# A SwiGLU layer in three token groups: sums of weight blocks and normed activations kept in device memory for later groups

## The chip, the cores and the metric

The kernel runs on one core of a Trainium2 chip. The metric is the time of the whole program on the device in microseconds (us); lower is better. Five engines work side by side and wait for each other through semaphores: TensorE (PE in the profile, with its weight loads as PEld), VectorE (DVE), ScalarE (ACT), GpSimd (POOL) and SyncE (SP), which here issues every DMA.

## The reference, cut to what matters

One layer over 2048 + 64 tokens with a width of 1024. The first part (a combined input projection, three mixers, an output projection) is the same in both kernels. The change lies in the second part, a SwiGLU feed-forward block over the result `x`:

```python
h2 = rms_norm(x, lw["ffn_norm"])                         # per token, gain per channel
ff = jax.nn.silu(h2 @ lw["w_gate"]) * (h2 @ lw["w_up"])  # 1024 -> 2816, twice
x = x + ff @ lw["w_down"]                                # 2816 -> 1024
```

Everything is fp32, and the outputs must be fp32-accurate.

## The kernel before, in words

**Arithmetic.** Each fp32 operand is split into a high part (a cast to the fp32r type, on ACT) and a low part, the difference (`rest` on POOL at L86 for weights, L1067 on DVE or POOL for activations). A product is three matmuls, high x high, high x low and low x high (`mm3`). The gate and up projections also use the Strassen-Winograd scheme: an output block pair of 2x2 blocks is made from 7 products instead of 8 (`seven`), each of a weight block or a sum of weight blocks (a11, s2, a12, s1, s3, s4, a22) with a block or a sum of blocks of the normed activations (b11, t2, b21, t1, t3, b22, t4). A product is 4 k steps of 3 matmuls of 128x352, so 84 matmuls make a projection for one pair.

**Loops.** The feed-forward block walks three token groups (`gi`, 704 tokens each) and, in each, 11 pairs of 128-wide blocks of the hidden width (`p`). For a pair the code writes `gate(p)` (84 matmuls), `DN(p-1)`, the down projection of the pair before (96), and `up(p)` (84); `DN(10)` comes last in its group. That is 264 matmuls for a pair and 2904 for a group.

**Weights.** `wsum(p, j)` (L1106 to L1131) is called for every gate (j = 0) and every up (j = 1) in every group. It loads two tiles of 512 KB from `w_gu` (L1109, tile `x2`, 3 buffers, shared with the down weights), forms s1, s3, s2 and s4 on DVE (L1121, L1122, L1123, L1128, in this order), and makes 7 pairs of a cast (L1114) and a rest (L86) into tiles `w` (8 buffers). The sum at L1128 overwrites a12, so it has to wait for the rest of a12 on POOL. `DN` loads 512 KB of down weights per half (L1207), casts it (L1209) and takes its rest (L86, 128x1024).

**Activations.** `HB` holds the seven activation blocks of one group as high and low parts, each 128 x 4 x 352, written in place for the next group. `H2(gi, k, ...)` fills the k-th quarter of all seven: two loads of 352 KB from `x1all` into the one buffer `xh` (L1058), two scalings on DVE (L1059), four sums on DVE (L1072 to L1078), seven casts on ACT (L1065) and seven lows on POOL and DVE (L1067). For groups 1 and 2 the four calls of H2 are written inside `DN(10)` of the group before, one ahead of each of its first four output blocks. Since a quarter goes into all seven blocks, a product of full depth needs all four calls.

**Evictions.** Sums of products leave PSUM on DVE (L1146, L1173, L1188), the up side is multiplied in at L1189 and split into `ah` and `al` (L1191 on ACT, L1192 on DVE), and each piece of the down projection is added into `acc` on DVE (L1221). PSUM gives `gu` 5 buffers and `dn` 3.

**Order.** A scheduler in the framework fixes the order of instructions on each engine when the program is built. Each engine then runs its own list in order, and SP issues the DMAs in order.

Of the kernel before, what the change touches and what calls it, by code (L numbers as in the profile page):

```python
# [3 lines left out]
def prm(n,d):  # L4
    return type(d)(PRM.get(n,d))
# [7 lines left out]
F32 = mybir.dt.float32  # L13
# [8 lines left out]
P = 128  # L22
# [27 lines left out]
def hybrid_layer(ctx: ExitStack, tc: tile.TileContext, x_all, x_t, w_in, w_out, w_gu, w_dn, par, gates, poolw,  # L50
# [56 lines left out]
    x1row = dram.tile([1, T], F32, name="x1row")  # L107

# [663 lines left out]
    ORD0 = "P0 A0 v0 P1 p0 S G0 m0 L0 p1 R0 L1 m1 l0 B0 n0 l1 A1 n1 b0 G1 A2 R1 B1 G2 A3 R2 b1 G3 X Q0 R3 Q1 q0 K0 u0 q1 K1 u1 k0 V w0 k1 w1 v"  # L772
    ORD1 = "A0 S G0 A1 R0 G1 A2 R1 B0 G2 A3 R2 B1 G3 X Q0 b0 R3 Q1 q0 b1 K0 u0 q1 K1 u1 k0 V w0 k1 w1 v"
    ORD3 = "A0 G0 A1 R0 G1 A2 R1 B0 G2 A3 R2 b0 B1 G3 b1 R3"
# [3 lines left out]
    def IN(g):  # L778
# [9 lines left out]
        o = PRM[o].replace("_", " ") if o in PRM else {"o0": ORD0, "o1": ORD1, "o3": ORD3}[o]  # L788
# [195 lines left out]
    def OUT(ci, last=None):  # L984
# [36 lines left out]
        def stat(ps=None, po=po):  # L1021
# [25 lines left out]
          for k in ("b11", "b21", "b22", "t1", "t2", "t3", "t4")}  # L1047
# [54 lines left out]
    def raw():  # L1102
        return pf.tile([P, 1024], F32, name="x2", bufs=3)

    def wsum(p, j):

        r = [raw(), raw()]
        for e in range(2):
            sp.dma_start(r[e], w_gu[2 * p + e, :, j, :])  # L1109
        a11, a12, a21, a22 = r[0][:, :512], r[0][:, 512:], r[1][:, :512], r[1][:, 512:]  # L1110

        def parts(src):
            w = pf.tile([P, 2, 512], F32R, name="w", bufs=prm("b_wg", 8))
            act.copy(w[:, 0, :], src)  # L1114
            rest(w[:, 1, :], w[:, 0, :], src)
            return w

        W = {}
        W["a11"] = parts(a11)
        s1 = pf.tile([P, 512], F32, name="s1", bufs=1)  # L1120
# [9 lines left out]
        W["a22"] = parts(a22)  # L1130
        return W  # L1131

# [35 lines left out]
    def gate(p):  # L1168
# [7 lines left out]
        seven(wsum(p, 0), use)  # L1176
        return s

    def up(p, s):
# [14 lines left out]
        seven(wsum(p, 1), use)  # L1194
        acts[p] = res

    for gi in range(3):
# [4 lines left out]
        def DN(p, extra=()):  # L1202
            extra = list(extra)
            for half in range(2):
                r = raw()
                src = w_dn[2 * p * P:(2 * p + 2) * P, half * 512:half * 512 + 512].rearrange("(q p) e -> p q e", p=P)
                sp.dma_start(r.rearrange("p (q e) -> p q e", q=2), src)  # L1207
                w = pf.tile([P, 2, 1024], F32R, name="wd", bufs=2)
                act.copy(w[:, 0, :], r)  # L1209
                rest(w[:, 1, :], w[:, 0, :], r)  # L1210
# [16 lines left out]
        for p in range(NF // 2):  # L1227
            s = gate(p)
# [4 lines left out]
            up(p, s)  # L1233
            if p == 0:
                sp.dma_start(acc, x1all[:, :, c0:c0 + GT].rearrange("k p t -> p k t"))
# [103 lines left out]
```

## Time and profile before

| | |
|---|---|
| time, median of 3 runs | 2549.59 us (2541.57 to 2551.30) |
| the profiled execution's own time | 2549.71 us |
| its span | 2547.9 us |
| mean granted TensorE clock | 0.954 of full speed |
| feed-forward block on PE | from 1042.5 us to the end |

The time of an execution is its span and 1.8 us around it. The profile has one line for a group of instructions on one engine at one source line, with the busy time, the mean duration of one, and the idle time of the engine just before them with what ended it. A wait is named "engine line <- releaser": the engine stood still at an instruction of this line until the releaser was done.

### The profile page before, as it was taken

The numbers are of one execution on the slowest core, as the hardware profiler recorded it, in microseconds if no ns is written. First come the engines' busy times: TensorE is split into PE (matmuls) and PEld (weight loads), VectorE is DVE, ScalarE is ACT, GpSimd is POOL, SyncE is SP. The second block draws the span as 40 slices with busy tenths as digits, with TensorE's granted clock in tenths as the row PEclk, the third lists the DMA queues.
The fourth block names the chain that finished last, engine by engine and source line by source line (L and its number), as shares of the span: only waits on it lengthen the run. The fifth ranks groups of instructions, "written<-read, shape, count | busy, mean of one in ns | idle before, by whom it ended". The sixth has DMA issues, their size and how long they took to land. (4 is left out here: it accounts for less than half of the span.)

```text
span 2547.9 us, 37616 instructions
## 1 busy us (share of the span) xinstructions
PE 2337.3 (92%) x14158; PEld 2212.8 (87%) x14158; DVE 1690.7 (66%) x2711; ACT 962.6 (38%) x1780; POOL 1097.4 (43%) x788
## 2 busy tenths in 40 slices
PE   5877898989989999899999997999999979999999
PEld 5875767778768999799999996999999979999999
DVE  4457377497789744476666687666676777666665
ACT  3435254355565422333333233323232333333331
POOL 3433013131121133565555555555565555555552
PEclk8888899999999999899999998999999989999999
DMA  7796575765746354422212124212222242222212
GB/s 265 204 256 214 164 241 182 223 197 181 227 129 183 110 152 126 143 92 67 83 63 83 63 90 158 85 60 83 66 75 75 81 153 82 75 75 67 83 60 78
DMA packets 169553, 324.38 MB, mean 127 GB/s; under 512 B 30444, under 2 KB 87643, under 8 KB 161435
## 3 DMA queue, kind: packets, MB, share of 16 engines
q1 hardware_dynamic: 169370, 321.98, 40.1%
q8 instruction: 112, 1.84, 0.3%
q14 instruction: 71, 0.57, 0.1%
HBM read 256.38 MB, written 63.37 MB: 125 GB/s over the span
## 5 line engine op out<-in xcount | busy, mean ns | idle before, releaser
L86 POOL TENSOR_TENSOR w<-x,w 128x512 fp32r<-128x512 f32 x396 | 545.1, 1396 | 533.0 <-ACT w L1114 520.7
L78 PE MATMUL dn<-ah,wd 128*128 128x352 f32 x2112 | 563.8, 326 | 38.2 <-DVE acc L1221 24.6
L78 PE MATMUL gu<-ht,w 128*128 128x352 f32 x2112 | 549.8, 325 | 0.0
L78 PE MATMUL mm<-hTh,w 128*128 128x512 f32 (+3 forms) x1632 | 444.6, 350 | 32.9 <-DVE raw L304 17.5
L78 PE MATMUL gu<-hb,w 128*128 128x352 f32 x1584 | 421.9, 327 | 35.5 <-ACT hb L1065 21.5
L1114 ACT CAST w<-x 128x512 fp32r<-128x512 f32 x396 | 238.2, 616 | 563.5 <-PE gu L78 308.8
L78 PEld LDWEIGHTS dn<-ah,wd 128*128 128x128 f32 x2112 | 378.6, 189 | 49.1 <-DVE acc L1221 33.6
L78 PEld LDWEIGHTS gu<-ht,w 128*128 128x128 f32 x2112 | 378.9, 190 | 0.9 <-ACT w L1114 0.8
L78 PEld LDWEIGHTS mm<-hTh,w 128*128 128x128 f32 x1632 | 297.9, 199 | 66.3 <-DVE raw L304 18.2
L78 PE MATMUL gu<-lt,w 128*128 128x352 f32 x1056 | 343.2, 326 | 0.1
L78 PE MATMUL dn<-al,wd 128*128 128x352 f32 x1056 | 342.5, 324 | 0.0
L1221 DVE TENSOR_TENSOR acc<-dn,acc 128x352 f32<-128x352 f32 x528 | 266.6, 520 | 104.7 <-PE dn L78 104.5
L78 PEld LDWEIGHTS gu<-hb,w 128*128 128x128 f32 x1584 | 287.0, 191 | 38.7 <-ACT hb L1065 23.0
L78 PE MATMUL mm<-hTl,w 128*128 128x512 f32 (+3 forms) x816 | 282.6, 347 | 0.0
L78 PE MATMUL gu<-lb,w 128*128 128x352 f32 x792 | 260.6, 329 | 4.3 <-POOL lb L1067 2.5
L78 PEld LDWEIGHTS gu<-lt,w 128*128 128x128 f32 x1056 | 200.2, 190 | 1.1 <-DVE lt L1067 0.6
L78 PEld LDWEIGHTS dn<-al,wd 128*128 128x128 f32 x1056 | 200.0, 189 | 1.0 <-DVE al L1192 1.0
L86 POOL TENSOR_TENSOR wd<-x,wd 128x1024 fp32r<-128x1024 f32 x66 | 164.5, 2493 | 69.6 <-ACT wd L1209 63.6
L78 PEld LDWEIGHTS mm<-hTl,w 128*128 128x128 f32 x816 | 162.4, 199 | 15.0 <-issue 2.2
L1189 DVE TENSOR_TENSOR s<-s,v 128x352 f32<-128x352 f32 x132 | 169.5, 1284 | 1.4
L657 DVE TENSOR_TENSOR_SCAN C<-z,C,zero 128x512 f32<-128x512 f32 (+4 forms) x148 | 160.2, 1087 | 10.6 <-ACT z L649 9.3
L78 PEld LDWEIGHTS gu<-lb,w 128*128 128x128 f32 x792 | 151.4, 191 | 8.2 <-POOL lb L1067 4.6
(243 smaller groups left out, 3709.6 us busy)
## 6 DMA issues: line engine op xcount, KB each, us to landing
x<-in_w_gu SPq DMA_DIRECT2D x132, 512.0 KB
w<-wk SPq DMA_DIRECT2D x46, 1024.0 KB
x<-in_w_dn SPq DMA_DIRECT2D x66, 512.0 KB
wk<-w SPq DMA_DIRECT2D x16, 1024.0 KB
V<-vscr SPq DMA_DIRECT2D x40, 256.0 KB
K<-kscr SPq DMA_DIRECT2D x40, 256.0 KB
xh<-x1all SPq DMA_DIRECT2D x24, 352.0 KB
acc<-x1all SPq DMA_DIRECT2D x3, 2816.0 KB
```

The lines of the kernel that those rows point to most:

```text
L78: pe.matmul(out, lhsT, rhs, start=start, stop=stop)
L86: gp.tensor_tensor(out, src, hi, ALU.subtract)
L657: dve.tensor_tensor_scan(C[:n, :w][:, ::-1], om[:n, :w][:, ::-1], zero1[:n].to_broadcast([n, w]), carry, ALU.mult, ALU.add)
L1114: act.copy(w[:, 0, :], src)
L1189: dve.tensor_tensor(o, o, v, ALU.mult)
L1221: dve.tensor_tensor(acc[:, d, a:b], ps[:, :HT], acc[:, d, a:b], ALU.add)
```

## The change

The change has four parts.

- **Weight sums.** In group 0 `wsum` loads four tiles of 256 KB (`x5`, 8 buffers, in place of `x2`), forms the four sums as before, and stores them to device memory (`wsc`, four stores of 256 KB). In groups 1 and 2 it loads seven tiles of 256 KB, three from `w_gu` and four from `wsc`, and forms no sum. The tile `w` goes from 8 to 7 buffers.
- **Down weights.** `DN` loads, casts and takes the rest of each half in two pieces of 128x512 instead of one of 128x1024.
- **Activations, mid-group.** `H2_sums(gi+1, k)` is written behind `up(p)` for p = 1, 3, 5 and 7: the same loads, scalings and sums as in H2, and seven stores of 176 KB to device memory (`hsc`).
- **Activations, change of group.** `H2_load(gi+1, n)` takes the place of the H2 calls inside `DN(10)`, once for each of the seven blocks, in the order in which the products need them: one load of 704 KB into one of two staging tiles (`xh`, `xg`, alternately), one cast of 128x1408 and one low of 128x1408 (DVE for four of them, POOL for three).

```diff
--- before.py
+++ after.py
@@ -105,6 +105,10 @@
     CH = [(i * 256, 256 + (NS if i == 3 else 0)) for i in range(SEQ // 256)]
     x1all = dram.tile([KD, P, T], F32, name="x1all")
     x1row = dram.tile([1, T], F32, name="x1row")
+
+    wsc = [[dram.tile([P, 4, 512], F32, name=f"wsc{p}_{j}") for j in range(2)] for p in range(NF // 2)]
+    BL = ("b11", "t2", "b21", "t1", "t3", "b22", "t4")
+    hsc = [None] + [{b: dram.tile([P, 4, T // 6], F32, name=f"hsc{g}{b}") for b in BL} for g in (1, 2)]
 
     cp = ctx.enter_context(tc.tile_pool(name="cp", bufs=1))
     ident = cp.tile([P, P], F32, name="ident")
...
@@ -1044,7 +1045,7 @@
     GT = T // 3
     HT = GT // 2
     HB = {k: (pr2.tile([P, 4, HT], F32R, name="h" + k), pr2.tile([P, 4, HT], F32R, name="l" + k))
-          for k in ("b11", "b21", "b22", "t1", "t2", "t3", "t4")}
+          for k in BL}
 
     def H2_row(gi):
         rb = pr2.tile([P, GT], F32, name="rb2")
@@ -1100,24 +1101,32 @@
         return psF.tile([P, 512], F32, name="gu", tag="gu", bufs=5)
 
     def raw():
-        return pf.tile([P, 1024], F32, name="x2", bufs=3)
-
-    def wsum(p, j):
-
-        r = [raw(), raw()]
-        for e in range(2):
-            sp.dma_start(r[e], w_gu[2 * p + e, :, j, :])
-        a11, a12, a21, a22 = r[0][:, :512], r[0][:, 512:], r[1][:, :512], r[1][:, 512:]
-
-        def parts(src):
-            w = pf.tile([P, 2, 512], F32R, name="w", bufs=prm("b_wg", 8))
-            act.copy(w[:, 0, :], src)
-            rest(w[:, 1, :], w[:, 0, :], src)
-            return w
+        return pf.tile([P, 512], F32, name="x5", bufs=prm("b_x5", 8))
+
+    def parts(src):
+        w = pf.tile([P, 2, 512], F32R, name="w", bufs=prm("b_wg", 7))
+        act.copy(w[:, 0, :], src)
+        rest(w[:, 1, :], w[:, 0, :], src)
+        return w
+
+    def wsum(gi, p, j):
+
+        def load(src):
+            r = raw()
+            sp.dma_start(r, src)
+            return r
+
+        def blk(e, h):
+            return load(w_gu[2 * p + e, :, j, h * 512:h * 512 + 512])
 
         W = {}
+        if gi:
+            for k, src in (("a11", (0, 0)), ("s2", 0), ("a12", (0, 1)), ("s1", 1), ("s3", 2), ("s4", 3), ("a22", (1, 1))):
+                W[k] = parts(blk(*src) if isinstance(src, tuple) else load(wsc[p][j][:, src, :]))
+            return W
+        a11, a21, a22, a12 = blk(0, 0), blk(1, 0), blk(1, 1), blk(0, 1)
         W["a11"] = parts(a11)
-        s1 = pf.tile([P, 512], F32, name="s1", bufs=1)
+        s1 = raw()
         dve.tensor_tensor(s1, a21, a22, ALU.add)
         dve.tensor_tensor(a21, a11, a21, ALU.subtract)
         dve.tensor_tensor(a11, s1, a11, ALU.subtract)
@@ -1128,7 +1137,37 @@
         dve.tensor_tensor(a12, a12, a11, ALU.subtract)
         W["s4"] = parts(a12)
         W["a22"] = parts(a22)
+        for i, t in enumerate((a11, s1, a21, a12)):
+            sp.dma_start(wsc[p][j][:, i, :], t)
         return W
+
+    flop = [0]
+
+    def hstage():
+        flop[0] ^= 1
+        return pr2.tile([P, 2, GT], F32, name="xh") if flop[0] else pf.tile([P, 2, GT], F32, name="xg")
+
+    def H2_sums(gi, k, rb):
+
+        xh, tt = hstage(), hstage().rearrange("p a t -> p (a t)").rearrange("p (b t) -> p b t", b=4)
+        for e in range(2):
+            sp.dma_start(xh[:, e, :], x1all[k + 4 * e][:, gi * GT:(gi + 1) * GT])
+            dve.scalar_tensor_tensor(xh[:, e, :], xh[:, e, :], gn2_sb[:, k + 4 * e:k + 4 * e + 1], rb, ALU.mult, ALU.mult)
+        b11, b12, b21, b22 = xh[:, 0, :HT], xh[:, 0, HT:], xh[:, 1, :HT], xh[:, 1, HT:]
+        t1, t2, t3, t4 = (tt[:, i, :] for i in range(4))
+        dve.tensor_tensor(t1, b12, b11, ALU.subtract)
+        dve.tensor_tensor(t3, b22, b12, ALU.subtract)
+        dve.tensor_tensor(t2, b22, t1, ALU.subtract)
+        dve.tensor_tensor(t4, b21, t2, ALU.subtract)
+        for n, t in (("b11", b11), ("b21", b21), ("b22", b22), ("t1", t1), ("t2", t2), ("t3", t3), ("t4", t4)):
+            sp.dma_start(hsc[gi][n][:, k, :], t)
+
+    def H2_load(gi, n):
+        st = hstage().rearrange("p a t -> p (a t)").rearrange("p (k t) -> p k t", k=4)
+        sp.dma_start(st, hsc[gi][n])
+        h, l = HB[n]
+        act.copy(h, st)
+        (gp if BL.index(n) % 2 else dve).tensor_tensor(l, st, h, ALU.subtract)
 
     def prod(W, b):
         ps = ps_gu()
@@ -1165,7 +1204,7 @@
 
     acts = {}
 
-    def gate(p):
+    def gate(gi, p):
         s = [pf.tile([P, GT], F32, name="s", bufs=3) for _ in range(2)]
 
         def use(i, x, y):
@@ -1173,10 +1212,10 @@
             dve.tensor_tensor(o, x, y, ALU.add)
             act.activation(o, o, AF.Silu)
 
-        seven(wsum(p, 0), use)
+        seven(wsum(gi, p, 0), use)
         return s
 
-    def up(p, s):
+    def up(gi, p, s):
         res = []
         for e in range(2):
             res.append((pf.tile([P, GT], F32R, name="ah", bufs=2), pf.tile([P, GT], F32R, name="al", bufs=2)))
@@ -1191,7 +1230,7 @@
             act.copy(ah[:, cs], o)
             dve.tensor_tensor(al[:, cs], o, ah[:, cs], ALU.subtract)
 
-        seven(wsum(p, 1), use)
+        seven(wsum(gi, p, 1), use)
         acts[p] = res
 
     for gi in range(3):
@@ -1202,12 +1241,13 @@
         def DN(p, extra=()):
             extra = list(extra)
             for half in range(2):
-                r = raw()
-                src = w_dn[2 * p * P:(2 * p + 2) * P, half * 512:half * 512 + 512].rearrange("(q p) e -> p q e", p=P)
-                sp.dma_start(r.rearrange("p (q e) -> p q e", q=2), src)
                 w = pf.tile([P, 2, 1024], F32R, name="wd", bufs=2)
-                act.copy(w[:, 0, :], r)
-                rest(w[:, 1, :], w[:, 0, :], r)
+                for q in range(2):
+                    r = raw()
+                    sp.dma_start(r, w_dn[(2 * p + q) * P:(2 * p + q + 1) * P, half * 512:half * 512 + 512])
+                    qs = slice(q * 512, q * 512 + 512)
+                    act.copy(w[:, 0, qs], r)
+                    rest(w[:, 1, qs], w[:, 0, qs], r)
                 w = w.rearrange("p s (q e) -> p s q e", q=2)
                 for d in range(4 * half, 4 * half + 4):
                     if extra:
@@ -1225,18 +1265,21 @@
                         sp.dma_start(y[d][:, c0:c0 + GT], acc[:, d, :])
 
         for p in range(NF // 2):
-            s = gate(p)
+            s = gate(gi, p)
             while pend:
                 pend.pop(0)(ps_gu(), pr2)
             if p:
                 DN(p - 1)
-            up(p, s)
+            up(gi, p, s)
             if p == 0:
                 sp.dma_start(acc, x1all[:, :, c0:c0 + GT].rearrange("k p t -> p k t"))
+            if gi < 2 and p in (1, 3, 5, 7):
+                if p == 1:
+                    rb2 = H2_row(gi + 1)
+                H2_sums(gi + 1, p // 2, rb2)
         extra = ()
         if gi < 2:
-            rb2 = H2_row(gi + 1)
-            extra = [lambda k=k, gi=gi, rb2=rb2: H2(gi + 1, k, rb2, 3) for k in range(4)]
+            extra = [lambda n=n, gi=gi: H2_load(gi + 1, n) for n in BL]
         DN(NF // 2 - 1, extra)
 
 
```

The changed order on PE at the first change of group, where `up(10)` of group 0 ends (`gu` is a gate or up product, `dn` a down product; in the kernel before hb_9437, ht_9441, ht_9445 and ht_9443 are the high parts of b21, t1, t3 and t2, lb and lt the low ones). Before, 19 rows behind the end of `up(10)`:

```order
L78 MATMUL dn<-ah,wd 128x352
L78 MATMUL gu<-ht_9443,w 128x352
L78 MATMUL gu<-hb_9437,w 128x352
L78 MATMUL gu<-lb_9438,w 128x352
L78 MATMUL gu<-hb_9437,w 128x352
L78 MATMUL gu<-ht_9441,w 128x352
L78 MATMUL gu<-lt_9442,w 128x352
L78 MATMUL gu<-ht_9441,w 128x352
L78 MATMUL gu<-ht_9445,w 128x352
L78 MATMUL gu<-lt_9446,w 128x352
L78 MATMUL gu<-ht_9445,w 128x352
L78 MATMUL dn<-ah,wd 128x352
```

After, from the first row behind the end of `up(10)` (hb_9471 is b11, ht_9473 is t2):

```order
L78 MATMUL gu<-hb_9471,w 128x352
L78 MATMUL gu<-lb_9472,w 128x352
L78 MATMUL gu<-hb_9471,w 128x352 x2
L78 MATMUL gu<-lb_9472,w 128x352
L78 MATMUL dn<-ah,wd 128x352
L78 MATMUL gu<-hb_9471,w 128x352 x2
L78 MATMUL gu<-lb_9472,w 128x352
L78 MATMUL gu<-hb_9471,w 128x352 x2
L78 MATMUL gu<-lb_9472,w 128x352
L78 MATMUL gu<-hb_9471,w 128x352
L78 MATMUL gu<-ht_9473,w 128x352
L78 MATMUL gu<-lt_9474,w 128x352
```

Before, one k step of each product of the new group stands between pieces of `DN(10)`, and nothing more. Now b11's product of all four k steps stands first and t2's follows, with single matmuls of `DN(10)` between them.

On SP, one pair of group 0. Before, the loads of one pair (two for the gate, two for the up, two for the down weights):

```order
L1109 DMA x_13225<-in_w_gu 128x1024
L1109 DMA x_13226<-in_w_gu 128x1024
L1109 DMA x_13375<-in_w_gu 128x1024
L1109 DMA x_13376<-in_w_gu 128x1024
L1207 DMA x_13511<-in_w_dn 128x2x512
L1207 DMA x_13580<-in_w_dn 128x2x512
```

After, the four loads of one up side (x_12569 to x_12575), ahead of them and between them the last store of the gate before (`wsc_0`), then the four stores of the up side's sums (`wsc_1`) with the first three loads of the next gate (the number behind `wsc` is the tile's own):

```order
L1116 DMA x_12569<-in_w_gu 128x512
L1141 DMA wsc_0_118<-x_12281 128x512
L1116 DMA x_12571<-in_w_gu 128x512
L1116 DMA x_12573<-in_w_gu 128x512
L1116 DMA x_12575<-in_w_gu 128x512
L1141 DMA wsc_1_119<-x_12580 128x512
L1116 DMA x_12744<-in_w_gu 128x512
L1141 DMA wsc_1_119<-x_12571 128x512
L1116 DMA x_12746<-in_w_gu 128x512
L1116 DMA x_12748<-in_w_gu 128x512
L1141 DMA wsc_1_119<-x_12569 128x512
L1141 DMA wsc_1_119<-x_12575 128x512
```

The stores of one `wsum` now stand between the loads of the next ones, and a load is issued only when the store in front of it has been.

On DVE, at the first change of group inside `DN(10)`. Before (the second quarter, k = 2, of the H2 calls; L1221 is an eviction of a down piece):

```order
L1078 TENSOR_TENSOR xh<-xh 128x352
L1067 TENSOR_TENSOR lt_9444<-xh,ht_9443 128x352
L1221 TENSOR_TENSOR acc<-dn,acc 128x352
L1059 SCALAR_TENSOR_TENSOR xh<-xh,gn_sb,rb_14657 128x704 x2
L1072 TENSOR_TENSOR xh<-xh 128x352
L1067 TENSOR_TENSOR lb_9438<-xh,hb_9437 128x352
L1074 TENSOR_TENSOR xh<-xh 128x352
L1067 TENSOR_TENSOR lt_9442<-xh,ht_9441 128x352
L1075 TENSOR_TENSOR xh<-xh 128x352
L1067 TENSOR_TENSOR lt_9446<-xh,ht_9445 128x352
L1078 TENSOR_TENSOR xh<-xh 128x352
L1067 TENSOR_TENSOR lt_9444<-xh,ht_9443 128x352
```

After, in `DN(10)` and the gate of pair 0 of group 1 (L1170 is the low of an H2_load, L1261 the eviction of a down piece, L1212 and L1185 evictions of gate products, L1155 to L1161 the scalings and sums of `H2_sums(2, 0)`, which the code writes behind `up(1)` of group 1):

```order
L1170 TENSOR_TENSOR lt_9484<-xh,ht_9483 128x1408
L1261 TENSOR_TENSOR acc<-dn,acc 128x352 x3
L1155 SCALAR_TENSOR_TENSOR xg<-xg,gn_sb,rb_15949 128x704
L1212 TENSOR_TENSOR s<-gu,c_15265 128x352
L1155 SCALAR_TENSOR_TENSOR xg<-xg,gn_sb,rb_15949 128x704
L1158 TENSOR_TENSOR xh<-xg 128x352
L1185 TENSOR_TENSOR u_15297<-gu,u_15267 128x352
L1159 TENSOR_TENSOR xh<-xg 128x352
L1160 TENSOR_TENSOR xh<-xg,xh 128x352
L1261 TENSOR_TENSOR acc<-dn,acc 128x352 x2
L1161 TENSOR_TENSOR xh<-xg,xh 128x352
L1261 TENSOR_TENSOR acc<-dn,acc 128x352
```

The scalings and sums of the quarters are gone from this place for group 1, the lows are whole blocks, and the first of the `H2_sums` for group 2 stand among the evictions. On SP the two loads of `x1all` for these sums stand four DMAs behind the last H2_load.

## Rows read from the trace of the kernel before

**Rows 1.** The page's busy time, share of the span and instructions by engine.

```profile
PE 2337.3 (92%) x14158; PEld 2212.8 (87%) x14158; DVE 1690.7 (66%) x2711; ACT 962.6 (38%) x1780; POOL 1097.4 (43%) x788
```

**Rows 2.** Windows: busy us (and instructions) of each engine, granted clock, DMA share, GB/s.

```profile
1042.00:1150.00 108.00, 102.47 (x602) 99.89 (x603) 72.90 (x107) 42.56 (x77) 72.83 (x51) 0.95 0.32 111
1150.00:1500.00 350.00, 344.80 (x2145) 342.76 (x2144) 231.75 (x373) 114.68 (x209) 192.63 (x128) 1.00 0.23 74
1500.00:1600.00 100.00, 78.19 (x419) 73.74 (x418) 78.71 (x113) 34.37 (x68) 51.83 (x36) 0.86 0.40 140
1600.00:2000.00 400.00, 390.99 (x2417) 387.79 (x2416) 264.27 (x423) 132.89 (x243) 224.70 (x151) 1.00 0.22 74
2000.00:2090.00 90.00, 70.76 (x388) 66.61 (x387) 67.48 (x101) 30.33 (x59) 40.71 (x30) 0.85 0.37 127
2090.00:2520.00 430.00, 421.32 (x2613) 417.69 (x2612) 287.50 (x457) 140.88 (x256) 239.86 (x159) 1.00 0.22 73
```

**Rows 3.** A window of 10 us at the first change of group, columns as above.

```profile
1540.00:1550.00 10.00, 3.79 (x11) 2.81 (x11) 5.49 (x9) 2.81 (x6) 2.46 (x3) 0.74 0.92 333
```

**Rows 4.** PE's waits, 1500 to 1600 us: us in total, times, longest.

```profile
PE gu L78 <- ACT hb L1065: 10.2, 2, 5.2
PE dn L78 <- ACT ah L1191: 5.0, 1, 5.0
PE gu L78 <- DVE u L1146: 3.8, 1, 3.8
```

**Rows 5.** PE's waits, 2010 to 2090 us.

```profile
PE gu L78 <- ACT hb L1065: 11.3, 2, 5.9
PE dn L78 <- ACT ah L1191: 5.1, 1, 5.1
```

**Rows 6.** Timeline of SP's DMA issues, 1500 to 1600 us: start, us, line, DMA, count.

```profile
1526.94 13.21 SPq L1225 DMA_DIRECT2D out_y<-acc  x6
1540.48 0.82 SPq L1058 DMA_DIRECT2D xh<-x1all  x2
```

**Rows 7.** Timeline of DVE, 1538 to 1562 us: start, us, operation, idle before, releaser.

```profile
1543.69 1.88 DVE L1059 SCALAR_TENSOR_TENSOR xh<-xh,gn_sb,rb 128x704 f32<-128x704 f32 x2 [3.90 <-DMA xh<-x1all]
1555.16 1.82 DVE L1059 SCALAR_TENSOR_TENSOR xh<-xh,gn_sb,rb 128x704 f32<-128x704 f32 x2 [4.48 <-DMA xh<-x1all]
```

**Rows 8.** The same wait of PE in 1150:1505, 1600:2010 and 2090:2548.

```profile
PE dn L78 <- DVE acc L1221: 5.2, 7, 1.6
...
PE dn L78 <- DVE acc L1221: 9.0, 11, 2.2
...
PE dn L78 <- DVE acc L1221: 8.0, 11, 1.2
```

**Rows 9.** Timeline of DVE in group 1, 1815 to 1832 us.

```profile
1819.29 1.76 DVE L1128 TENSOR_TENSOR x<-x 128x512 f32<-128x512 f32 x1 [2.46 <-POOL w L86]
...
1827.47 0.69 DVE L1121 TENSOR_TENSOR s<-x 128x512 f32<-128x512 f32 x1 [3.71 <-DMA x<-in_w_gu]
```

**Rows 10.** DVE's wait for weights, 1150 to 1505 us (group 0).

```profile
DVE s L1121 <- DMA x<-in_w_gu: 26.6, 8, 4.6
```

**Rows 11.** Groups by shape, 1042 to 2548 us: busy us, mean ns, idle before.

```profile
L1189 DVE TENSOR_TENSOR s<-s,v 128x352 f32<-128x352 f32 x132 | 169.5, 1284 | 1.4
L1188 DVE TENSOR_TENSOR v<-gu,u 128x352 f32<-128x352 f32 x99 | 51.3, 518 | 1.6 <-PE gu L78 0.5
L1123 DVE TENSOR_TENSOR x<-s,x 128x512 f32<-128x512 f32 x66 | 45.3, 686 | 2.8
L1128 DVE TENSOR_TENSOR x<-x 128x512 f32<-128x512 f32 x66 | 94.9, 1437 | 80.6 <-POOL w L86 80.6
L1114 ACT CAST w<-x 128x512 fp32r<-128x512 f32 x396 | 238.2, 616 | 563.5 <-PE gu L78 308.8 <-DVE x L1123 198.5 <-DVE x L1128 31.3
L86 POOL TENSOR_TENSOR w<-x,w 128x512 fp32r<-128x512 f32 x396 | 545.1, 1396 | 533.0 <-ACT w L1114 520.7 <-DMA x<-in_w_gu 6.6 <-PE gu L78 3.7
L86 POOL TENSOR_TENSOR wd<-x,wd 128x1024 fp32r<-128x1024 f32 x66 | 164.5, 2493 | 69.6 <-ACT wd L1209 63.6 <-PE gu L78 4.0
```

More of the change, by code (lines that the diff above doesn't have):

```diff
@@ L770, in X_Q @@
         return us
-    ORD0 = "P0 A0 v0 P1 p0 S G0 m0 L0 p1 R0 L1 m1 l0 B0 n0 l1 A1 n1 b0 G1 A2 R1 B1 G2 A3 R2 b1 G3 X Q0 R3 Q1 q0 K0 u0 q1 K1 u1 k0 V w0 k1 w1 v"
-    ORD1 = "A0 S G0 A1 R0 G1 A2 R1 B0 G2 A3 R2 B1 G3 X Q0 b0 R3 Q1 q0 b1 K0 u0 q1 K1 u1 k0 V w0 k1 w1 v"
-    ORD3 = "A0 G0 A1 R0 G1 A2 R1 B0 G2 A3 R2 b0 B1 G3 b1 R3"
     WT = {"A": 5.2, "G": 5.1, "R": 0.9, "B": 5.2, "b": 0.4, "X": 1.0, "S": 0.0,
@@ L787, in IN @@
         o = "o0" if g == 0 else "o3" if g == NG - 1 else "o1"
-        o = PRM[o].replace("_", " ") if o in PRM else {"o0": ORD0, "o1": ORD1, "o3": ORD3}[o]
+        o = PRM[o].replace("_", " ")
         for tok in o.split():
```

## The prediction

> **What bounds the kernel now.** I read the page's totals first: PE is busy 92% of the span, DVE 66%, POOL 43% [rows 1]. So the question is where PE stands still in the part that the change touches, and the windows by stage answer it. In the steady part of group 0 (1150 to 1500 us) PE runs 2145 instructions in 344.80 busy us, 6.22 per us or 0.16 us each at full clock [rows 2]. I divide each window's count by that rate and take the result from its length:
>
> 1042 to 1150: 602 / 6.22 = 96.8, lost 11.2 us.
> 1150 to 1500: lost 5.2.
> 1500 to 1600: 419 / 6.22 = 67.4, lost 32.6.
> 1600 to 2000: 2417 / 6.22 = 388.5, lost 11.5.
> 2000 to 2090: 388 / 6.22 = 62.4, lost 27.6.
> 2090 to 2520: 2613 / 6.22 = 420.0, lost 10.0.
>
> In all 98 us are lost, and 60 of them lie at the two changes of group. There PE's own waits say what ends last: at the first change 10.2 us for the cast of a new b block (L1065), 5.0 for `ah`, 3.8 for a sum of products [rows 4]; at the second 11.3 and 5.1 [rows 5]. That is 19.0 and 16.4; the other 13.6 and 11.2 are short waits and the lower clock, 0.86 and 0.85 in these windows, 0.74 in the worst one [rows 2, 3].
>
> The cast waits for the scaling, and the scaling for its load. SP spent 13.21 us over six stores of `acc` pieces, each waiting for its eviction, and only then issued the next loads, at 1540.48 [rows 6]; DVE began the scaling at 1543.69, after 3.90 us without work, and the next quarter at 1555.16, 11.5 us later [rows 7]. The quarters run one behind the other because `xh` is one buffer, and no product of full depth can be made before the last. PE has nothing else to run. In that window it is busy 3.79 us of 10, DMA 92% [rows 3].
>
> The rest of the loss recurs: PE waits for `acc` evictions for 5.2, 9.0 and 8.0 us in groups 0, 1 and 2 [rows 8]. The timeline shows why: DVE, in order, stands 2.46 us at L1128 for POOL and 3.71 us at L1121 for a weight load, with evictions behind both [rows 9].
>
> **The change part by part.** The number of matmuls stays 14008, so only the waits can move.
>
> *Change of group.* Group 1's sums are made hundreds of us earlier. What is left per block is a load of 704 KB, a cast and a low. The load: two loads of together 704 KB took 3.2 us from issue (1540.48) to their first use (1543.69) [rows 6, 7]. The cast: 616 ns for 512 columns [rows 11], so at most 616 x 2.75 = 1.7 us for 1408. The low: on POOL 1396 x 2.75 = 3.8 us, or 2493 x 1.375 = 3.4 from the wider form; on DVE from 686 x 2.75 = 1.9 us to 4.7, if it suffers like L1189, 1284 against 518 ns of L1188 for the same shape [rows 11]. A step is 6.8 to 9.6 us, four on one staging tile and three on the other, and the first load of each is issued far ahead, early in group 0. Counted from the start of `up(10)`, b11 is free after its product of 12 x 0.16 = 1.9 us, and the fourth step on its tile ends at 1.9 + 1.7 + 4.7 + 3 x 9.6 = 37 us at the latest. PE needs that block, t4, after `up(10)` and `DN(9)` (180 matmuls, 28.9 us) and 126 more, at 49 us. Earlier blocks come out alike; with evictions ahead of the lows on DVE I leave at least 8 us of margin. The 5 us for `ah` go too: one to two full products of the new gate now stand ahead of `DN(10)`, where there were three matmuls.
>
> What is late next at the first change is `H2_sums(2, 0)`, whose scalings stand among the evictions of `DN(10)`. Their load needs a staging tile that the last H2_loads hold; by the steps above it lands between 30 and 36 us, and the evictions behind it are wanted near 42. I leave 8 us lost here (bounds 2 and 20), and 4 at the second change (1 and 10), which has no such sums. Gain 32.6 - 8 + 27.6 - 4 = 48.
>
> *Groups 1 and 2, steady.* Four DVE sums per `wsum` go, and with them both of DVE's waits of [rows 9]. Of the 17.0 us for `acc` [rows 8] I take 14 as gained (bounds 8 and 20). DMA grows: 22 x 7 + 44 loads of 256 KB are 52 MB in some 467 us (2904 x 0.16), 111 GB/s against 74 now at a DMA share of 0.22 [rows 2], so a share near 0.33. POOL's down rests become two of 1396 instead of one of 2493 ns, 0.3 us each; POOL has 175 us idle in 400 [rows 2].
>
> *Group 0.* Two additions. The order of after puts all four `H2_sums` for group 1 at the start of the block: each two scalings (1.88 us [rows 7]) and four sums of 0.52 [rows 11], 4.0 us of DVE, 16 together, where DVE is busy 72.9 of 108 us and PE loses 11.2 already [rows 2]: +4 (bounds 0 and 16). And the stores of sums stand ahead of later loads on SP. DVE waits for weights there 26.6 us in eight waits now [rows 10], and PE loses only 5.2, so some delay is covered; I take 0.2 us for each of 22 `wsum`, +4 (bounds 0 and 77, see below). Splitting the down load and going from 8 to 7 `w` buffers I cost at nothing: a `wsum` has seven parts, and POOL makes one in 1.4 us where PE uses one in 1.9; without that slack it would be 0.5 us a part.
>
> The sum: -48 - 14 + 8 = -54. The profiled execution took 2549.7 us, as long as the median of the runs, so 2496.
>
> **The rivals.**
>
> *A, the sum above:* 2480 to 2510 us, chance 0.53.
>
> *B, DVE gives part of it back,* 0.21. The sums of `H2_sums` have both operands in SBUF, as L1189 has, which takes 0.77 us more than L1188 [rows 11]. With 16 such sums at the start of group 0 and 16 at the start of group 1, among evictions, this is 32 x 0.77 = 24 us: 2520, with a range of 2510 to 2537. For it: DVE is busy 78.7 of 100 us at the first change already [rows 2]. Against it: in the steady part DVE is idle for 118 of 350 us [rows 2], and PSUM's buffers let an eviction come late by some us. The Trainium skill (SBUF — State Buffer, Who interferes with whom) says that such an instruction with two SBUF inputs and a GpSimd one that reads SBUF lock each other out for a whole instruction. By that rule each sum could wait for a rest of 1.4 us, an estimate of 45 us and 2541; the trace agrees with the direction, 1284 against 518 ns, and its mean is below the rule's worst case.
>
> *C, everything goes:* the two changes and the steady waits vanish and group 0 costs nothing: 2549.7 - 32.6 - 27.6 - 17 = 2472, 2465 to 2480. Chance 0.08.
>
> *D, the change of group does not improve:* the casts must wait for PE's last read of each block and the staged chain ends too late, so that PE loses its 60 us as before, only in other places. Then -14 + 8: 2544, 2537 to 2562. Against it is the margin of 8 us or more. Chance 0.10.
>
> *E, slower:* in group 0 SP stops at a store, which waits for its sum, which at L1128 waits for POOL; the loads behind it come late, DVE stands at L1121 longer, and evictions behind it hold PE. If that costs 3.5 us per `wsum`, the longest kind of wait seen now [rows 9], 22 x 3.5 = 77 us: 2573. It cancels the gain from 54 / 22 = 2.5 us per `wsum`. For it: eight waits in 350 us mean 3.3 us each [rows 10]. Against it: PE pays a fifth of them today, and the eight smaller buffers let the next `wsum` load before the last is used up. Chance 0.08.
>
> **How the numbers follow.** A measurement of this kernel can tell about 0.5%, 12.7 us, from no change: below 2537 is faster, above 2562 slower. A, B and C end below, 0.82; D within, 0.10; E above, 0.08. The likeliest is A's sum, 2496, with its own range 2480 to 2510. A range of 2474 to 2540 takes in A, B, most of C and the lower edge of D, 0.82 in all.
>
> **What would show it.** In the profile after: PE's wait for the casts of new blocks gone, and full clock, in the windows of both changes; no wait of PE for `acc` in groups 1 and 2; DVE's sums of weights in group 0 alone; DMA share near 0.33 there. B would show as waits of PE for `acc` or gate sums at the start of groups 0 and 1, with DVE in scalings and sums just before. E would show as longer waits of DVE for weights in group 0, with SP's stores ahead of the loads. The prediction is wrong if PE waits for H2_load's casts or lows, or if group 0's steady part loses more than some 10 us.

## Result and the profile after

The changed kernel took 2474.8 us (median of 4 runs, 2468.2 to 2480.2), the kernel before 2550.5 (4 runs). The ratio is 0.9708, 95% interval 0.9674 to 0.9742: faster by 2.9%, or some 75 us, where the prediction had 54. In a second set of rounds it was 2469.9 us, ratio 0.9685 (0.9667 to 0.9703). 2496 was forecast; 2474.8 lies inside the range of 2474 to 2540 by less than a us, and 2469.9 lies below it. Both lie outside case A's own 2480 to 2510 and in the 2465 to 2480 of case C. The profiled execution's span is 2473.9 us, 74.0 less than before.

The page's busy times after, to set against [rows 1]:

```profile
PE 2310.0 (93%) x14158; PEld 2199.7 (89%) x14158; DVE 1569.1 (63%) x2511; ACT 964.4 (39%) x1804; POOL 1120.2 (45%) x836
```

The windows by stage of the changed kernel, columns as in [rows 2]. The second change of group now lies near 2000 us, astride two windows:

```profile
1042.00:1150.00 108.00, 96.47 (x562) 93.00 (x563) 91.58 (x117) 40.99 (x78) 74.97 (x52) 0.94 0.79 255
1150.00:1500.00 350.00, 350.00 (x2189) 350.00 (x2188) 243.00 (x378) 120.92 (x231) 210.53 (x149) 1.00 0.41 127
1500.00:1600.00 100.00, 95.33 (x570) 93.41 (x569) 79.48 (x111) 35.37 (x62) 65.91 (x42) 0.97 0.84 279
1600.00:2000.00 400.00, 396.76 (x2469) 396.08 (x2468) 226.28 (x362) 147.83 (x272) 244.07 (x173) 1.00 0.39 121
2000.00:2090.00 90.00, 90.00 (x564) 90.00 (x564) 47.44 (x80) 33.22 (x63) 53.40 (x41) 1.00 0.56 182
2090.00:2470.00 380.00, 379.23 (x2371) 378.59 (x2370) 205.39 (x348) 122.46 (x233) 199.79 (x148) 1.00 0.33 104
```

The second row is a stretch in which PE never waits: 2189 instructions in 350 us, 6.254 per us. The first matmul of the feed-forward block is at 1042.53 us before and at 1042.95 after, so the windows at its start compare. With this rate for both kernels the losses (length less count / 6.254) are, before [rows 2] and after:

| stage | before, us | after, us |
|---|---|---|
| start of group 0 (1042 to 1150) | 11.7 | 18.1 |
| rest of group 0 (1150 to 1500) | 7.0 | 0 |
| both changes (1500 to 1600 and 2000 to 2090; after, with 1600 to 2000) | 61.0 | 13.9 |
| steady part of groups 1 and 2 | 25.7 | 0.9 |

The differences are -6.4, +7.0, +47.1 and +24.8, together 72.5 of the 74.0 us. PE's waits at the first change of group (1500 to 1600 us), which answer to [rows 4]:

```profile
PE dn L78 <- DVE al L1231: 3.1, 2, 2.5
PE gu L78 <- DVE u L1185: 1.1, 1, 1.1
PE dn L78 <- DVE acc L1261: 0.3, 1, 0.3
```

Nothing waits for a new block any more: of 19.0 us in three waits 4.5 are left, none of them for a cast or a low of a new block. In 1150 to 1490 and 1600 to 1955 us the view of PE's waits is empty, where [rows 8] had 5.2 and 9.0 us.

The new blocks came in time, though their loads took longer than forecast. The last of them, t4, from its issue on SP to its cast on ACT:

```profile
1511.09 0.32 SPq L1167 DMA_DIRECT2D xh<-hsc1t  x1
...
1517.50 1.37 ACT L1169 CAST ht<-xh 128x1408 fp32r<-128x1408 f32 x1 [0.79 <-DMA xh<-hsc1t]
```

That is 6.4 us, where the prediction had 3.2 for a load. The casts of the four blocks on `xh` begin 9.3, 10.2 and 11.4 us apart, where a step was to take 6.8 to 9.6. The low of t4 is done at 1522.9 us, 41.6 us behind the start of `up(10)`, where 37 was to be the latest. PE comes to t4's product, 126 matmuls behind the end of `up(10)`, only at 1536.8.

### The profile page after: what moved, and what is told of

Read it like the earlier page. It is cut to its first block, busy times and chain, and to the rows that moved or that the text cites. A ratio compares the mean times of both kernels' runs of the same rounds, so it can differ in the third digit from the quotient of the medians.

```text
span 2473.9 us, 38503 instructions
## 1 busy us (share of the span) xinstructions
PE 2310.0 (93%) x14158; PEld 2199.7 (89%) x14158; DVE 1569.1 (63%) x2511; ACT 964.4 (39%) x1804; POOL 1120.2 (45%) x836
## 4 chain that ended last, share of the span: by engine, by line
PE 66%; DMA 14%; DVE 10%; issue 4%; ACT 2%; SPq 2%; POOL 2%; ACTq 0%; DVEq 0%; POOLq 0%
PE gu L78 32%; PE dn L78 20%; PE mm L78 10%; DVE C L661 1%; PE av L78 1%; PE z L78 1%; DMA wk<-w 1%; PE tp L705 1%; DMA vtscr<-vT 1%; DMA vp<-vf 1%; DMA q<-qscr 1%; DVE xc L533 1%; DMA mix<-r 1%; DMA qscr<-hl 1%; DVE aTl L707 1%
## 5 line engine op out<-in xcount | busy, mean ns | idle before, releaser
L86 POOL TENSOR_TENSOR w<-x,w 128x512 fp32r<-128x512 f32 x462 | 638.8, 1396 | 508.7 <-ACT w L1108 493.1
L78 PE MATMUL dn<-ah,wd 128*128 128x352 f32 x2112 | 548.0, 324 | 6.6 <-ACT ah L1230 3.4
L1108 ACT CAST w<-x 128x512 fp32r<-128x512 f32 x462 | 279.4, 619 | 520.8 <-PE gu L78 294.1
L78 PE MATMUL mm<-hTh,w 128*128 128x512 f32 (+3 forms) x1632 | 441.8, 348 | 36.4 <-DVE raw L308 18.3
L78 PE MATMUL gu<-hb,w 128*128 128x352 f32 x1584 | 416.7, 324 | 8.5 <-ACT w L1108 7.9
L1261 DVE TENSOR_TENSOR acc<-dn,acc 128x352 f32<-128x352 f32 x528 | 273.0, 522 | 217.8 <-PE dn L78 217.2
L86 POOL TENSOR_TENSOR wd<-x,wd 128x512 fp32r<-128x512 f32 x132 | 192.1, 1474 | 54.7 <-ACT wd L1249 54.6
L1185 DVE TENSOR_TENSOR u<-gu,u 128x352 f32<-128x352 f32 x132 | 68.8, 521 | 129.1 <-PE gu L78 128.7
```

Source lines behind the costliest of these rows:

```text
L78: pe.matmul(out, lhsT, rhs, start=start, stop=stop)
L86: gp.tensor_tensor(out, src, hi, ALU.subtract)
L1185: add = lambda o, x, y: dve.tensor_tensor(o, x, y, ALU.add)
L1261: dve.tensor_tensor(acc[:, d, a:b], ps[:, :HT], acc[:, d, a:b], ALU.add)
```

## Experiments

Each kernel was timed beside the kernel before on the same chip, and a ratio is against that. The first part of the program has the same code in all kernels, but the feed-forward block behind it begins at 1032.5 to 1043.9 us in the profiled executions, so a window with fixed ends at the start of group 0 holds more or less of the block. Where it matters I give the block's own length, from its first matmul to the end of the span: 1505.4 us before, 1430.9 and 1431.2 in two profiles of the changed kernel.

**Which part gives what.** Four kernels take the change apart.

`e1_sums_again`: no kept sums; loads, buffers and activations stay as changed.

```diff
         W = {}
-        if gi:
-            for k, src in (...): W[k] = parts(...)
-            return W
...
-        for i, t in enumerate((a11, s1, a21, a12)):
-            sp.dma_start(wsc[p][j][:, i, :], t)
```

> The changed kernel, but groups 1 and 2 load the four weight blocks and form the four sums on VectorE again, as group 0 does; nothing is stored to or read from the kept sums. Theory L (the steady waits went because the weights come as four tiles of 256 KB into eight buffers, so that loads run ahead): within 6 us of the changed kernel, 2470 to 2481 us, and TensorE does not wait for evictions of down pieces in the steady part of groups 1 and 2, as it does not in group 0 now. Theory S (they went because VectorE has no sums left to stand at): the waits of 9.0 and 8.0 us and their small change are back, some 21 us more, 2490 to 2500 us.

2484.0 us, ratio 0.9751 (0.9727 to 0.9774). Its windows (1150 to 1480 and 1600 to 1940 us):

```profile
1150.00:1480.00 330.00, 330.00 (x2064) 330.00 (x2063) 230.85 (x360) 112.66 (x221) 197.90 (x142) 1.00 0.26 76
1600.00:1940.00 340.00, 340.00 (x2127) 340.00 (x2126) 236.99 (x371) 115.14 (x224) 201.71 (x144) 1.00 0.25 76
```

PE is busy all the time in group 1 although DVE forms all sums again (237 busy us, 184 in the changed kernel in the same window). So theory S falls for the steady part: the sums can stay and the waits go all the same. The kernel is still some 9 us slower than the changed one (11 by the ratios), 3 outside of theory L's range, and the trace has those at the changes of group. PE's waits in 1490 to 1600 us:

```profile
PE dn L78 <- DVE acc L1254: 5.0, 2, 3.4
PE dn L78 <- ACT ah L1223: 3.5, 2, 1.9
PE dn L78 <- DVE al L1224: 1.9, 1, 1.9
PE gu L78 <- DVE u L1178: 0.7, 1, 0.7
```

11.1 us against 4.5. So the kept sums are worth something at the changes, where DVE also has lows, splits and evictions to do, and nothing between them.

`e2_h2_old`: changed weights, activations made at the change as before.

```diff
-            if gi < 2 and p in (1, 3, 5, 7):
...
-                H2_sums(gi + 1, p // 2, rb2)
...
-            extra = [lambda n=n, gi=gi: H2_load(gi + 1, n) for n in BL]
+            rb2 = H2_row(gi + 1)
+            extra = [lambda k=k, gi=gi, rb2=rb2: H2(gi + 1, k, rb2, 3) for k in range(4)]
```

> The changed weights (sums kept, split loads), with the normed blocks of the next group made at the change of group as in the kernel before. If the 46 us at the two changes come from the activations alone: 2475 + 46 - 6 (the start of group 0 has no sums of activations any more) = 2515 us, 2508 to 2523, with TensorE waiting some 10 us at each change for the casts of the new blocks. Rival (the freed VectorE and the smaller loads relieve the change of group as well): under 2505 us, with less than half of those waits.

2502.8 us, ratio 0.9830 (0.9806 to 0.9855). The waits for casts of new blocks are back, 10.1 us at the first change and 8.9 at the second, so the change of the activations is what removes them. At the first change:

```profile
PE gu L78 <- ACT hb L1065: 10.1, 2, 7.6
```

But the time is 5 us under the first theory's range and just inside the rival's, whose sign, less than half of those waits, is not there; and the waits for `ah` are 2.0 and 2.3 us where [rows 4, 5] have 5.0 and 5.1. The new weights relieve the changes a little too.

`e3_h2_only`: the kernel before with `H2_sums` and `H2_load` in place of H2, weights untouched.

> The kernel before with the activations alone changed (sums of the next group kept in device memory mid-group, seven loads at the change); weights as before, in tiles of 512 KB and with sums in every group. If the parts add up: 2550 - 46 + 6 = 2510 us, 2502 to 2518; TensorE's waits for evictions of down pieces in the steady parts stay at 5, 9 and 8 us, VectorE's wait for weight loads stays near 26 us in 340. Rival (the old loads stall the new activations, since VectorE stands at the weight sums with scalings behind them): above 2520 us, with waits for the new blocks at the changes.

2530.7 us, ratio 0.9935 (0.9913 to 0.9957), 13 us above the range. The steady waits stay as expected (7.4 and 6.8 us for `acc` in 330 and 340 us), and no new block is waited for, so neither theory had it right. PE's waits at its first change (1480 to 1600 us):

```profile
PE gu L78 <- DVE u L1177: 5.7, 1, 5.7
PE dn L78 <- ACT ah L1222: 4.6, 1, 4.6
PE dn L78 <- DVE acc L1252: 2.4, 3, 1.3
PE dn L78 <- DVE al L1223: 1.4, 1, 1.4
```

With the old weights the `ah` wait keeps its 5 us and DVE's evictions come late as well. The activations alone give 17 us, on top of the new weights some 30 (ratio 0.9830 in `e2_h2_old`, 0.9708 in the changed kernel). Most of what is missing is lost at the start of group 0 (1042 to 1150 us):

```profile
1042.00:1150.00 108.00, 93.65 (x536) 89.18 (x535) 75.00 (x107) 37.22 (x67) 64.08 (x43) 0.93 0.50 167
```

PE runs 536 instructions where [rows 2] have 602, although this block began 3.6 us earlier, at 1038.9. Its longest wait there is 5.2 us for the cast of a down weight (`wd`), which points to weights that come late beside the loads and stores of `H2_sums`.

`e4_loads_only`: `e1_sums_again` and `e2_h2_old` together, so that only the loads, their buffers and the split down weights differ from before.

> The kernel before with nothing but the loads changed: weights in four tiles of 256 KB into eight buffers, down weights in two pieces, seven buffers for the split weights; sums formed in every group and not kept, normed blocks at the change of group as before. Theory L: the steady losses of all three groups go, 2550 - 30 = 2520 us, 2512 to 2527, and VectorE's wait for weight loads in group 0 falls from 26 us to near 0. Theory S: only group 0's 5 us go, 2545 us, 2540 to 2550.

2510.8 us, ratio 0.9859 (0.9840 to 0.9878), faster than theory L's range by a us. The stretch of group 0 and DVE's wait in it:

```profile
1150.00:1480.00 330.00, 330.00 (x2064) 330.00 (x2064) 231.25 (x359) 113.30 (x223) 196.45 (x142) 1.00 0.25 76
```

```profile
DVE x L1131 <- POOL w L86: 20.0, 8, 2.5
```

DVE's wait for weight loads, 26.6 us in [rows 10], is gone; its wait for POOL at the last sum is there in full, and PE loses nothing to it. Half of the whole gain is in how raw weights are loaded.

The four kernels side by side with before and after, counted matmul by matmul from the block's first (8712 in all, the last 62 left out), so that the different starts do not matter. The loss of a stretch is its time less its matmuls / 6.254:

| matmuls | before, us | `e3_h2_only` | `e2_h2_old` | `e4_loads_only` | `e1_sums_again` | after |
|---|---|---|---|---|---|---|
| 0 to 600, start of group 0 | 11.9 | 29.2 | 9.8 | 8.3 | 16.1 | 17.9 |
| 600 to 2500, rest of group 0 | 7.3 | 6.1 | 0.2 | 0.2 | 0.2 | 0.2 |
| 2500 to 3400 and 5400 to 6300, the changes and what is around them | 69.1 | 33.1 | 54.5 | 64.6 | 28.2 | 14.9 |
| 3400 to 5400 and 6300 to 8650, rest of groups 1 and 2 | 20.2 | 20.0 | 1.4 | 1.8 | 1.8 | 1.3 |
| length of the block | 1505.4 | 1485.0 | 1462.3 | 1471.5 | 1443.1 | 1430.9 |

At the changes the new activations are worth 36 us alone and 40 on top of the new weights. At the start of group 0 they cost 17 us with the old weights and 8 with the new ones. The new weights, without the new activations, are worth 15 us around the changes.

**Room or smaller pieces.** Two kernels change only the number of buffers.

`e6_six_buffers`, on the changed kernel:

```diff
-        return pf.tile([P, 512], F32, name="x5", bufs=prm("b_x5", 8))
+        return pf.tile([P, 512], F32, name="x5", bufs=prm("b_x5", 6))
```

> The changed kernel with six tiles of 256 KB for raw weights instead of eight, 1.5 MB as much as the three tiles of the kernel before. Theory R (the steady waits went because eight tiles let loads run ahead): VectorE's waits for weight loads and TensorE's for evictions return in group 0, 2485 to 2505 us. Theory P (they went because a block can be used as soon as its own 256 KB are there): within 6 us of the changed kernel, 2469 to 2481.

2502.3 us, ratio 0.9822 (0.9806 to 0.9839), in theory R's range. In group 0 (1150 to 1480 us), PE's wait, then DVE's for loads:

```profile
PE dn L78 <- DVE acc L1261: 20.1, 14, 5.0
```

```profile
DVE x L1130 <- DMA x<-in_w_gu: 18.3, 6, 3.7
```

The room is less than before, though, not equal: s1 now takes one of the six tiles, where it had its own before, and in group 0 a tile is held until its store has read it. And in group 1 (1600 to 1940 us), where no sums are formed or stored, six tiles are enough:

```profile
PE dn L78 <- DVE acc L1261: 0.6, 2, 0.3
```

The kernel before has 8.4 us of this wait in the same window. So the waits also stay away when the sums go and the room does not grow.

`e8_four_tiles`, on the kernel before:

```diff
-        return pf.tile([P, 1024], F32, name="x2", bufs=3)
+        return pf.tile([P, 1024], F32, name="x2", bufs=4)
...
-            w = pf.tile([P, 2, 512], F32R, name="w", bufs=prm("b_wg", 8))
+            w = pf.tile([P, 2, 512], F32R, name="w", bufs=prm("b_wg", 7))
```

> The kernel before with four tiles of 512 KB for raw weights instead of three and seven buffers for split weights instead of eight, everything else as it was. Theory R (room to load ahead is what counts): the steady waits for evictions go, 2549 - 30 = 2519 us, 2512 to 2530. Theory P (the cut into 256 KB is what counts): 2543 to 2555, with the waits of 5, 9 and 8 us as before.

2526.4 us, ratio 0.9920 (0.9900 to 0.9940). Its two windows:

```profile
1150.00:1480.00 330.00, 330.00 (x2059) 329.09 (x2058) 230.67 (x356) 111.82 (x205) 191.34 (x126) 1.00 0.24 75
1600.00:1940.00 340.00, 338.97 (x2111) 337.93 (x2112) 238.19 (x370) 114.50 (x209) 195.86 (x128) 1.00 0.24 75
```

With 2 MB of raw tiles instead of 1.5 and the same pieces of 512 KB, PE waits for no eviction in this stretch of group 0 and 2.2 us in that of group 1, and the time is 19 us less than that of the kernel before beside it. DVE's wait for loads is gone from both, and its wait for POOL is still there, 20.1 us in group 0. So in the steady part it is room to load ahead that counts. It is not all of `e4_loads_only`, whose ratio is better by 0.006, some 15 us: around the changes this kernel loses 77 us, by the count of the table above, where `e4_loads_only` loses 65. Whether the smaller loads, the split down weights or s1's tile make that difference was not tried.

**The staging at the change.** `e7_one_stage` loads all seven blocks through one tile.

```diff
-        st = hstage().rearrange("p a t -> p (a t)").rearrange("p (k t) -> p k t", k=4)
+        st = pr2.tile([P, 2, GT], F32, name="xh").rearrange("p a t -> p (a t)").rearrange("p (k t) -> p k t", k=4)
```

> The changed kernel with one staging tile for the seven loads at the change of group instead of two. By the prediction's steps of 6.8 to 9.6 us the seven then take 48 to 67 us one behind the other and TensorE needs the last at 49 us, so it waits up to 18 us at each change: 2495 us, 2478 to 2515, with waits for lows or casts of t3, b22 or t4. Rival (the steps are much shorter than that, and two tiles are not needed): 2470 to 2480.

2473.2 us, ratio 0.9710 (0.9695 to 0.9724): no change that the time can tell (the block lasts 1434.5 us, 3.6 more). The steps were not short, though. The first and the last of its seven casts on ACT at the first change:

```profile
1481.26 1.38 ACT L1169 CAST hb<-xh 128x1408 fp32r<-128x1408 f32 x1
...
1533.78 1.37 ACT L1169 CAST ht<-xh 128x1408 fp32r<-128x1408 f32 x1 [4.57 <-DMA xh<-hsc1t]
```

Six steps in 52.5 us are 8.8 each, inside the predicted 6.8 to 9.6. What moved is PE's order: in this kernel's list t4's product begins 162 matmuls behind the end of `up(10)`, not 126, since the scheduler put 36 more matmuls of `DN(10)` ahead of it. Even so there is no margin: t4's cast ends at 1535.15 us and its first matmul begins at 1535.21, and at the second change PE waits 1.0 us for a cast. In the changed kernel's order PE would have come to it some 5.8 us sooner (an estimate, 36 / 6.254) and waited. So one tile is enough here only because the order moved.

**What the sums of activations cost.** In the changed kernel, `H2_sums` for group 1 stand at the start of group 0. DVE's timeline there, up to the eviction for which PE waited (columns as in [rows 9]):

```profile
1080.52 1.61 DVE L1231 TENSOR_TENSOR al<-s,ah 128x352 fp32r<-128x352 f32 x1
1082.06 1.98 DVE L1155 SCALAR_TENSOR_TENSOR xh<-xh,gn_sb,rb 128x704 f32<-128x704 f32 x1
1083.96 1.77 DVE L1137 TENSOR_TENSOR x<-x,x 128x512 f32<-128x512 f32 x1
1085.66 1.59 DVE L1231 TENSOR_TENSOR al<-s,ah 128x352 fp32r<-128x352 f32 x1
1087.17 1.95 DVE L1155 SCALAR_TENSOR_TENSOR xh<-xh,gn_sb,rb 128x704 f32<-128x704 f32 x1
1089.05 1.58 DVE L1231 TENSOR_TENSOR al<-s,ah 128x352 fp32r<-128x352 f32 x1
1090.55 1.58 DVE L1158 TENSOR_TENSOR xg<-xh 128x352 f32<-128x352 f32 x1
1092.05 0.51 DVE L1185 TENSOR_TENSOR u<-gu,c 128x352 f32<-128x352 f32 x1
```

```profile
1092.71 0.63 PE L78 MATMUL gu<-ht,w 128*128 128x352 f32 x1 [5.68 <-DVE u L1185]
```

DVE works without a gap, at 1.58 us for a 128x352 sum and 1.98 for a scaling, where 0.51 and 0.94 are their shortest times in this kernel; PE waits 5.68 us for the eviction. Three of the rows ahead of it are `H2_sums` (L1155 twice and L1158), 5.5 us together. This is the worst stretch: on average the sixteen sums for group 1 took 0.90 us each and the eight scalings 1.34.

`e5_sums_held` holds them where the code writes them.

```diff
-                H2_sums(gi + 1, p // 2, rb2)
+                with behind("dve", "sp"):
+                    H2_sums(gi + 1, p // 2, rb2)
```

> The changed kernel with the sums of activations held at the place where the code writes them, behind the pairs 1, 3, 5 and 7 of a group, on VectorE and SyncE; the work is the same. Theory H (the scheduler's early place costs: the start of group 0 loses 24 us in the changed kernel, 8 us where there are no such sums, and the first change loses 9 against 5.5 at the second): 16 + 3 = 19 us less, 2456 us, 2450 to 2464. Rival (that loss is the start's heavier store and load traffic, or the sums cost the same in the middle of the group): 2468 to 2480, with new waits in the middle of the groups.

2474.7 us, ratio 0.9713 (0.9698 to 0.9727): the rival. The start improves, by 4 us in the first 600 matmuls (598 instructions against 560 in the 106 us from 1044 overstate it, since this block began at 1032.5), but in the middle of group 0 (1150 to 1480 us) PE waits for evictions in three places:

```profile
PE dn L78 <- DVE acc L1261: 7.4, 3, 2.5
```

The block lasts 1436.8 us, 6 more than in the changed kernel, and yet the sums themselves took only 0.51 us in twelve of sixteen cases: which points to their place in blocks as the cost here.

`after_again` is the changed kernel in the rounds of the next two runs.

> The changed kernel itself, on the chip and in the rounds of the two runs below, to compare them with: 0.971 of the kernel before, 2474 us.

`e9_sums_spread` cuts the sums into single operations, each ahead of one output block of a down projection.

```diff
-                H2_sums(gi + 1, p // 2, rb2)
+                more = H2_parts(gi + 1, p // 2, rb2)
...
-                DN(p - 1)
+                DN(p - 1, more)
```

> The changed kernel with the sums of activations cut into single operations, one ahead of each output block of the down projections of pairs 1, 3, 5 and 7, held there on VectorE. Theory H2 (what costs is not the work but where it stands: heaped at the start of group 0 it costs 16 us there, in blocks of six operations behind a pair it costs 12 us in the middle of the group): both losses go, 2474 - 14 = 2460 us, 2454 to 2466. Rival (four to seven us more of VectorE in a pair of group 0, where it forms weight sums too, cost the same wherever they stand): 2470 to 2478.

2458.6 us, ratio 0.9656 (0.9637 to 0.9674), against 2469.9 and 0.9685 (0.9667 to 0.9703) for the changed kernel beside it. The intervals overlap by a hair, but the profile has what was expected: the block lasts 1418.0 us, 13 less than in both profiles of the changed kernel. Start and rest of group 0:

```profile
1044.00:1150.00 106.00, 103.47 (x639) 102.33 (x638) 80.19 (x118) 40.46 (x77) 76.45 (x55) 1.00 0.58 181
1150.00:1480.00 330.00, 330.00 (x2062) 330.00 (x2062) 241.73 (x374) 114.97 (x222) 200.43 (x140) 1.00 0.47 151
```

639 instructions in 106 us, where the changed kernel's second profile has 576 from nearly the same start of the block (1038.0 and 1038.7 us), and no loss in the middle. In the first 600 matmuls it loses 8.0 us, the changed kernel 17.9. This is the fastest kernel of the study.

`e10_late_stores` is `e9_sums_spread` with the sums of the first two pairs neither stored nor read.

```diff
-        if gi:
+        if gi and p > 1:
...
-        for i, t in enumerate((a11, s1, a21, a12)):
+        for i, t in enumerate((a11, s1, a21, a12) if p > 1 else ()):
```

> The kernel of the run above, and the weight sums of the first two pairs are formed again in every group and neither stored nor read, so that no store stands ahead of loads in the first 90 us of group 0 and fewer bytes move at the changes. Theory T (stores and loads crowd the start of group 0: its loss is 24 us in the changed kernel and 16 without stores): some 4 us less than the run above, 2456 us, 2450 to 2462. Rival (the VectorE sums of the first pairs of a group delay evictions at the changes, as where all sums were formed again): 4 to 8 us more than the run above.

2469.5 us, ratio 0.9687 (0.9674 to 0.9700), 11 us more than the run above: the rival. PE's waits at its first change (1480 to 1600 us):

```profile
PE dn L78 <- ACT ah L1241: 3.5, 2, 1.9
PE dn L78 <- DVE al L1242: 2.5, 1, 2.5
```

6.0 us, and 5.4 at the second change, against 3.2 and 3.3 in `e9_sums_spread`. Its block lasts 10 us more, of the 12 that `e1_sums_again` lost against the changed kernel: the kept sums of the first two pairs are the ones that pay. The start of group 0 was no better without stores (633 instructions in 106 us). My figure of 24 us for its loss had counted in the first wait of the block, 6.7 us for the first weights; all kernels have this wait, at 6.7 to 8.4 us.

## Why the prediction was right, and where it was off

- **The number: inside by luck.** Case A's sum missed by 21 us, and it was the wide range, not the sum, that took the result in, by 0.8 us. The time is that of case C, but C's account did not happen either: the changes still lose 13.9 us, the start of group 0 lost more than before, and the steady parts gave more than C had for them.
- **The changes of group: the wait was right, the sum in part by luck.** 48 us were forecast and 47 came. PE no longer waits for a new block, the granted clock rose from 0.86 and 0.85 to 0.97 and 1.00, and `e2_h2_old` has the waits back. But the forecast gave all of it to the activations, which measure 36 us alone and 40 on top of the new weights; the rest came with the weights, to which the prediction gave nothing at the changes. Of a step of H2_load the cast has the predicted size, 1.37 us (at most 1.7 forecast), and so nearly has the low, 1.94 on DVE (1.9 to 4.7) and 3.2 to 3.5 on POOL (3.4 to 3.8). The load does not: 6.4 us where 3.2 were taken, so a step took up to 11.4 us. The margin held because PE came to t4 14 us behind its low, where at least 8 were forecast. The `ah` wait of 5.0 us is gone at the first change and 2.7 at the second.
- **The steady part of groups 1 and 2: the term that was off.** "Four DVE sums per `wsum` go, and with them both of DVE's waits" gave 14 us of 17. It measured 24.8, and the reason given is not needed: `e1_sums_again` and `e4_loads_only` form all the sums and lose nothing there. Of the two waits in [rows 9] the one for the load hurt PE; the one for POOL is still 20 us in group 0 and costs nothing. The load came late for want of a free raw tile: `e8_four_tiles` gives one more and the wait is gone. The reason is not refuted either, since in group 1 of `e6_six_buffers` the waits stay away without more room, where the sums are gone. Either of the two is enough there, and the prediction had put no gain on the eight tiles. I had also counted only waits named for `acc`, and the losses that I had worked out from a rate with its own waits in it were too low.
- **Group 0: the sign was off.** I took 8 us as lost, 4 of them in the steady part for the stores. The start lost 6.4 more (4 forecast), by the mechanism of rival B, sums and scalings among evictions; `e9_sums_spread` takes this loss away with the same work in other places. The steady part gained 7.0, since the eight tiles help there too, 11 us better than forecast. With the 10.8 of groups 1 and 2 that is 21.8; the start was 2.4 worse and the changes 1 worse than forecast, which leaves 18.4 of the 20 us by which the span beats the forecast. The rest lies outside of these windows.
- **Rival E** (stores ahead of loads) did not happen: the wait of DVE's weight sums for loads is gone in the rest of group 0, and at the start 3.0 us of 18.3 are left. **Rival D** fell with the second point. **Rival B** was right on the place at the start of group 0 and too large in price: the sums took 0.39 us more than their shortest time on average, not 0.77, and at the start of group 1 PE waits 1.1 us for a gate sum. The Trainium skill's rule of the locked port pair (SBUF — State Buffer, Who interferes with whom) agrees in direction: in DVE's timeline above 128x352 operations with two SBUF inputs take 1.58 to 1.61 us, while the eviction with one PSUM input takes 0.51. That POOL's instructions cause it was not tried by itself.
- **DMA share.** I expected 0.33 in groups 1 and 2; it is 0.39 and 0.33. The count of PE's matmuls is 14158 in both kernels [rows 1], not 14008; no term rests on it.

What stays open: why `e3_h2_only` keeps the `ah` wait that goes when the loads change, and why the start of group 0 costs it 17 us; I read the first as later evictions and splits on DVE and the second as weights that come late, but no run changes either alone.

## What to carry to other kernels

When an in-order engine waits for two things, a trace of before need not tell which of the two holds up the bound engine; here a run with one more raw tile did. Ask of a change that removes work and also changes buffers which of the two the gain belongs to: here the way the weights are loaded carries half of it, the fourth tile by itself a quarter, and the removed sums add to that only at the changes, where DVE has most to do. A sum of terms can come out right while its terms are exchanged, so undo the parts one by one and compare each stretch from the same instruction. Work that is moved off a crowded place is best spread as single operations; as a block it cost elsewhere here what it saved.

## What the runs showed of the hardware

Loading the same bytes in pieces of 256 KB instead of 512 KB did no harm: in `e4_loads_only` PE is busy 330.00 of 330 us with 12 loads for each pair, at a DMA share of 0.25, against 0.23 before. And the traffic of the first change, 279 GB/s over 100 us at a DMA share of 0.84, against 140 and 0.40 before [rows 2], leaves PE the 4.5 us of waits shown above, none of them for weights or new blocks. The same 128x352 sum of two SBUF operands took from 0.51 to 1.58 us on DVE at the start of group 0.
